# Queries, keys, values and four gate tiles of a hybrid encoder layer as seven block products

## The chip, the cores and the metric

The kernel runs on one core of a Trainium2 chip. The core has five engines with instruction streams of their own: TensorE (PE, matrix products into PSUM), VectorE (DVE), ScalarE (ACT), GpSimd (POOL) and SyncE (SP, which here only issues transfers). Work is handed from engine to engine by semaphores, and each engine runs its own instructions in order. The metric is device microseconds of one execution; 1734.17 us is the median of three runs of the kernel before (1733.97 to 1736.21).

## The reference

One layer runs over 1024 prompt tokens and 32 sample tokens, all in float32. What matters here is its first half:

```python
ada = silu(c) @ w_ada + b_ada             # six vectors of 1024; the first two make shift and gain
h = rms_norm(x, g_pre_mix) * (1 + sc1) + sh1
p = h @ w_in                              # 1024 x 4256
q_lat, c_kv, k_r, q_b, k_b, v_b, g_a, g_b = split(p)   # 384, 256, 32, 3 x 512, 2 x 1024
o_b = stick_breaking(q_b, k_b, v_b)       # 8 heads of 64, strictly causal, by a product scan
o_a = latent_attention(q_lat, c_kv, k_r)  # softmax
merged = sigmoid(g_a) * (o_a @ w_proj_a) + sigmoid(g_b) * (o_b @ w_proj_b)
```

Then follow an output projection, a residual, a convolutional feed-forward network and a second residual. The keys and values of both groups of tokens are outputs too.

## The kernel before

**Precision.** A float32 matrix is split into a high part that PE takes in one pass (`hi`, L65, an ACT copy) and the rest (`lo`, L68, a DVE subtraction). A product is then three matmuls: high by high, high by low, low by high (`mm3`, L72 to L74). "Tokens" below are the 1056 columns of the transposed activations, 1024 of the prompt and 32 of the sample.

**The opening** (`stage_h`). Eight tiles of x (128 tokens by 1024) and the 8 MB of `w_ada` for the first two vectors come in over SP's queue: the shift and gain for the first 512 features (`ada_half(0)`), then for the second 512 (`ada_half(1)`), each from eight loads of 512 KB. The pool for them has eight buffers, and the last two loads of the second half take buffers of the weight pool. ACT squares x (L105), POOL makes the reciprocal root (L97, L98), DVE scales x (L344). `norm_T` turns four tiles of x at a time by PE transposes (L281), applies gain and shift on ACT while it evacuates PSUM (L287), and makes the high and low parts on DVE (L290, L291). The result is kept whole: `hh` and `hl`, 8 blocks of 128 features by 1056 tokens.

**Projections.** `w_in_tile` loads 128 columns of `w_in` (512 KB) and splits them. `mtile` then runs 8 feature blocks by three token blocks of 352 (`BLK`) by three matmuls, 72 matmuls for one column tile.

**Stick-breaking attention** (`stage_sb`, `sb_pair`). For each of four pairs of heads there are three column tiles: queries, keys, values. The high and low parts of queries and keys go straight into the tiles the scores read; keys and values are also turned back to natural order (L400) and stored as outputs, and the values' parts are made from that. Then `sb_attend` runs the two heads by `ORDER`, a list of steps written out by hand: scores (`S`), two sigmoids on ACT (`a`, `e`), a product scan on DVE (`c`), a product on DVE (`x`), transposes (`T`), their high and low parts (`h`, `v`) and the product with the values (`V`). Between these, `f` is one step of a filler, `gates`: four gate tiles for each pair, three matmuls of 352 columns for one `f`, and now and then a step that multiplies a block of `w_ada` (`ada_step`, L203) for the four vectors wanted later. `G` copies a finished gate block out, `W` and `w` split the next gate weights, `D` is a late piece of ada.

**What sets the order.** Outside of written blocks a planner orders each engine's instructions at build time, by program order and by what it believes to be ready. Inside a written block (`manual_schedule`) PE, ACT and DVE keep the order of the text; POOL and SP are still planned, and instructions from outside the block may be put between. A pool with `bufs=n` lets n tiles of one tag live at a time; the instruction that fills the next one waits until the oldest is no longer read.

**The neighbours.** `stage_lat` projects the latent columns with `mtile`; softmax attention, merge, up projection (`stage_up`) and down projection follow. The up projection is already done by seven block products: L1687 to L1689 are its matmuls, with token blocks of 256 and 272.

## Time and profile before

| | |
|---|---|
| median of three runs | 1734.17 us |
| the profiled execution | 1733.63 us |
| its span, first to last instruction | 1731.5 us |
| TensorE busy in the span | 1691.4 us, 98%, 11518 matmuls |
| VectorE, ScalarE, GpSimd busy | 1207.4, 911.7, 283.9 us |
| bytes moved | 223.62 MB, 129 GB/s on the mean |
| first score matmul of each head pair, from the span's start | 83.1, 199.6, 321.9, 437.1 us |

The busy time of PE is the union of its matmuls, each with its latency, so a row of matmuls that follow each other without a gap is 100% busy whatever its rate. Stretches are given in microseconds from the first instruction.

### The profile page before, as it was taken

The numbers are of one execution on the slowest core, as the hardware profiler recorded it, in microseconds if no ns is written. First come the engines' busy times: TensorE is split into PE (matmuls) and PEld (weight loads), VectorE is DVE, ScalarE is ACT, GpSimd is POOL, SyncE is SP. The second block draws the span as 40 slices with busy tenths as digits, with TensorE's granted clock in tenths as the row PEclk, the third lists the DMA queues.
The fourth block names the chain that finished last, engine by engine and source line by source line (L and its number), as shares of the span: only waits on it lengthen the run. The fifth ranks groups of instructions, "written<-read, shape, count | busy, mean of one in ns | idle before, by whom it ended". The sixth has DMA issues, their size and how long they took to land. (4 is left out here: it accounts for less than half of the span.)

```text
span 1731.5 us, 29721 instructions
## 1 busy us (share of the span) xinstructions
PE 1691.4 (98%) x11518; PEld 1542.4 (89%) x11518; DVE 1207.4 (70%) x1971; ACT 911.7 (53%) x1748; POOL 283.9 (16%) x586
## 2 busy tenths in 40 slices
PE   6999999999999999999999999999999999999998
PEld 3899999999999988989889789999999999977886
DVE  4576574673663687767786679887787787778456
ACT  5454453553554666766784286444444444544442
POOL 2211110211120011101100043211111121110013
PEclk8999999999999999999999999999999999999999
DMA  8343333333342222222345531534323323697743
GB/s 322 90 132 96 108 107 97 106 113 92 112 122 68 65 65 64 75 59 68 138 143 175 184 130 37 165 104 129 129 92 128 128 92 128 212 334 248 241 147 121
DMA packets 170093, 223.62 MB, mean 129 GB/s; under 512 B 12917, under 2 KB 117056, under 8 KB 169952
## 3 DMA queue, kind: packets, MB, share of 16 engines
q1 hardware_dynamic: 154336, 177.91, 32.4%
q0 software_dynamic: 15392, 43.74, 7.1%
q8 instruction: 90, 1.47, 0.4%
q14 instruction: 51, 0.42, 0.1%
q10 hardware_dynamic: 224, 0.09, 0.0%
HBM read 169.92 MB, written 51.25 MB: 128 GB/s over the span
## 5 line engine op out<-in xcount | busy, mean ns | idle before, releaser
L65 ACT ACTIVATE wh<-wr 128x1024 fp32r<-128x1024 f32 (+6 forms) x158 | 133.8, 856 | 249.6 <-PE s L1688 78.8
L68 DVE TENSOR_TENSOR wl<-wr,wh 128x1024 fp32r<-128x1024 f32 (+5 forms) x155 | 152.7, 991 | 139.6 <-ACT wh L65 139.0
L72 PE MATMUL mm<-hh,wh 128*128 128x352 f32 x688 | 231.6, 337 | 0.0
L73 PE MATMUL mm<-hl,wh 128*128 128x352 f32 x688 | 224.2, 326 | 0.4 <-DVE hl L291 0.3
L74 PE MATMUL mm<-hh,wl 128*128 128x352 f32 x688 | 224.2, 326 | 0.0
L72 PEld LDWEIGHTS mm<-hh,wh 128*128 128x128 f32 x688 | 130.0, 189 | 9.0 <-issue 4.9
L73 PEld LDWEIGHTS mm<-hl,wh 128*128 128x128 f32 x688 | 130.0, 189 | 3.9 <-DVE hl L291 1.8
L74 PEld LDWEIGHTS mm<-hh,wl 128*128 128x128 f32 x688 | 129.7, 189 | 0.8 <-issue 0.8
L68 DVE TENSOR_TENSOR PTl<-tr,PTh 128x512 fp32r<-128x512 f32 x100 | 68.3, 687 | 50.3 <-ACT PTh L65 49.9
L1689 PE MATMUL s<-T,wl 128*128 128x256 f32 (+1 forms) x328 | 93.6, 285 | 0.0
L1687 PE MATMUL s<-T,wh 128*128 128x256 f32 (+1 forms) x328 | 93.2, 284 | 0.0
L1688 PE MATMUL s<-T,wh 128*128 128x256 f32 (+1 forms) x328 | 93.2, 284 | 0.0
L1828 DVE SCALAR_TENSOR_TENSOR u<-u,c,u 128x1058 f32<-128x1058 f32 x68 | 87.0, 1317 | 2.0 <-ACT u L1825 0.7
L65 ACT ACTIVATE PTh<-tr 128x512 fp32r<-128x512 f32 x100 | 59.4, 598 | 53.5 <-PE tr L591 50.8
L591 PE MATMUL tr<-c,A 128*128 128x128 f32 x576 | 83.6, 274 | 0.6 <-DVE A L693 0.5
L1689 PE MATMUL tr<-T,wl 128*128 128x272 f32 (+1 forms) x272 | 77.6, 285 | 0.4 <-DVE wl L68 0.4
L1687 PE MATMUL tr<-T,wh 128*128 128x272 f32 (+1 forms) x272 | 77.9, 287 | 0.0
L1688 PE MATMUL tr<-T,wh 128*128 128x272 f32 (+1 forms) x272 | 77.5, 285 | 0.0
L68 DVE TENSOR_TENSOR wl<-S,wh 128x1024 fp32r<-128x1024 f32 x40 | 48.9, 1223 | 37.4 <-ACT wh L65 36.2
L591 PEld LDWEIGHTS tr<-c,A 128*128 128x128 f32 x576 | 68.1, 140 | 5.9 <-issue 1.6
L1689 PE MATMUL mm<-T,wl 128*128 128x256 f32 (+1 forms) x256 | 73.0, 286 | 0.3 <-DVE wl L68 0.2
L1687 PE MATMUL mm<-T,wh 128*128 128x256 f32 (+1 forms) x256 | 73.1, 286 | 0.0
(694 smaller groups left out, 5391.4 us busy)
## 6 DMA issues: line engine op xcount, KB each, us to landing
wr<-in_w_ada_dram SPq DMA_DIRECT2D x48, 512.0 KB, 4.6
wr<-in_w_up_dram SPq DMA_DIRECT2D x44, 512.0 KB, 4.2
dr<-in_w_down_dram SPq DMA_DIRECT2D x43, 512.0 KB, 5.9
wr<-in_w_in_dram SPq DMA_DIRECT2D x33, 512.0 KB, 4.6
wr<-gdn SPq DMA_DIRECT2D x30, 512.0 KB, 4.2
gdn<-u POOLq DMA_DIRECT2D x23, 512.0 KB, 5.3
gd<-nat POOLq DMA_DIRECT2D x48, 176.0 KB, 2.3
t<-gd SPq DMA_DIRECT2D x16, 528.0 KB, 6.3
```

Of the source, the lines that this page charges most:

```text
L65: self.nc.scalar.activation(out, in_, AF.Identity, scale=scale)
L68: return self.nc.vector.tensor_tensor(out, full, hi.bitcast(F32), ALU.subtract)
L72: m(ps, lh, rh, start=start, stop=False)
L73: m(ps, lh, rl, start=False, stop=False)
L74: self.pe = m(ps, ll, rh, start=False, stop=stop).ins
L591: self.nc.tensor.transpose(tr[:, (2 * s + q) * P : (2 * s + q + 1) * P], at[q][:, b * P : b * P + P], self.idt)
L1687: m(ps[:, :n], w[0][:, k], x[0][:, k, c], start=first and k == 0, stop=False, skip_group_check=True)
L1688: m(ps[:, :n], w[0][:, k], x[1][:, k, c], start=False, stop=False, skip_group_check=True)
L1689: i = m(ps[:, :n], w[1][:, k], x[0][:, k, c], start=False, stop=k == 3, skip_group_check=True)
L1828: nc.vector.scalar_tensor_tensor(y, u[:, w : w + YW], self.cvT[:, w, cc : cc + 1], y, ALU.mult, ALU.add)
```

## The change

Sixteen column tiles of `w_in`, twelve for queries, keys and values and four gate tiles, are taken in eight pairs (`PAIRS`). For one pair the weights are a 2 by 2 block matrix (two column tiles by two halves of 512 features), and so are the activations (two halves of features by two halves of 528 tokens, `B11`, `B12`, `B21`, `B22`). The 2 by 2 by 2 block product takes seven products of blocks in place of eight, with sums of weight blocks (`sum_1`, `sums_w`, `sum_4`) and sums of activation blocks (`T1` to `T4`). One product has 4 feature blocks, two token blocks of 256 and 272 columns (`Z_BLK`) and three matmuls each: 24.

The first two pairs (`g0`: two gate tiles; `g1`: queries and keys of head pair 0) run in the opening, in a written order in two blocks, one in `stage_h` and one in `stage_in`. The products that need the first 512 features alone stand ahead of `ada_half(1)`. The other six pairs run in `stage_in`, outside of a written block. All four head pairs' queries, keys and values are made there, ahead of the attentions; their high and low parts go to scratch in device memory (`z_done`) and come back for each pair (`sb_load`), all on POOL's queue. `B12` is kept as plain float32 in scratch during this, and split when the last pair is done.

The attentions follow each other without projections between; the filler now has the remaining twelve gate tiles, three for each attention, with four token blocks of 264 (`HBLK`), and `ORDER` is another list. It has 104 `f` steps as before. The latents take blocks of 264 too.

Smaller edits: `ada_half` takes its weights from five buffers; the load of b_ada stands behind that of its weights; some zero fills and copies move from DVE to POOL; the rope table is loaded after the first attention; the late vectors are made in `stage_in`.

```diff
     def ada_half(self, hf, wp, tp):
...
-            last = hf == 1 and k >= KT - 2
-            w = self.tl(*((self.W, [P, 1024]) if last else (wp, [P, 2 * 512])), F32, "wr").rearrange("p (v n) -> p v n", v=2)
+            w = self.tl(wp, [P, D], F32, "wr", 5).rearrange("p (v n) -> p v n", v=2)
...
+    def norm_T(self, t0, xs, tp, hf):
...
+        if t0 < 8:
+            edge = self.tl(tp, [P, 4, 16], F32, "edge") if t0 else None
+            for k in range(4):
...
+                put(f, x, q)
+                if H:
+                    put(H[0][:, k, c], x, q)
+                    self.lo(H[1][:, k, c], f, H[0][:, k, c])
+                if t0:
+                    put(edge[:, k], tr[:, 0:16], q)
...
     def stage_h(self):
...
+            g0, g1 = self.group(0), self.group(1)
+            with tc.manual_schedule(engines={E.PE, E.Activation, E.DVE}):
+                self.ada_half(0, wp, tp)
+                self.raw_a(g0)
+                for t in range(4, 8):
+                    load(t)
+                self.raw_a(g1)
+                nc.vector.tensor_scalar(xs, xs, self.rstd_s(xs, tp), None, ALU.mult)
+                n = norm(0, 0)
+                each(n, n)
+                wa = self.unit(g0["ra"][:, :512])
+                each(n, n)
+                for t in range(4, 8):
+                    scale(t)
+                each(norm(8, 0))
+                wb = []
+
+                def later(b):
+                    if b:
+                        return
+                    n = norm(4, 0)
+                    each(n, n, n, n)
+                    for i in range(2):
+                        nc.gpsimd.dma_start(self.f12d[i], self.F[0][i])
+                        x = self.F[1][i]
+                        self.plus(x, self.F[0][i], B11, i, ALU.subtract)
+                        if i == 0:
+                            wb.append(self.unit(g1["ra"][:, :512]))
+                        self.both(T1, x, i)
+
+                g0["q1"] = self.z_q("q1", 3)
+                self.z_out(g0["q1"], self.z_prod(wa, B11, "mm mm", then=later))
+                wa, = wb
+                g1["q1"] = self.z_q("q1", 3)
+                self.z_out(g1["q1"], self.z_prod(wa, B11, "mm mm"))
+                self.ada_half(1, wp, tp)
+                self.raw_b(g0)
+                self.raw_b(g1)
+                n, m = norm(0, 1), norm(4, 1)
+                each(n, n)
+                w = [self.unit(self.sum_1(g0))]
+                each(n)
+                w.append(self.unit(self.sum_1(g1)))
+                for g, t in ((g0, "mm mm"), (g1, "s pv")):
+                    b = self.z_prod(w.pop(0), T1, t, then=lambda i: each(n if g is g0 else m))
+                    self.out_b(g, b)
+                    self.sums_w(g)
+                    w.append(self.unit(g["ra"][:, 512:]))
...
+                        self.z_half(x, B21, b, g["Y"][b], True)
...
+    def raw(self, g):
+        return self.tl(self.W, [P, 1024], F32, "wr") if g["n"] % 2 == 0 else self.tl(self.Zq, [P, 1024], F32, "S", 2)
...
+    def unit(self, x):
+        if self.n_unit % 2 == 0:
+            self.wt = [self.tl(self.W, [P, 1024], F32R, t) for t in ("wh", "wl")]
+        i = 512 * (self.n_unit % 2)
+        self.n_unit += 1
+        h, l = (t[:, i : i + 512] for t in self.wt)
+        self.hi(h, x)
+        self.lo(l, x, h)
...
+    def z_half(self, w, x, b, ps, new):
+        c0, n = self.Z_BLK[b]
+        for k in range(4):
+            for i, (p, q) in enumerate(((0, 0), (0, 1), (1, 0))):
+                self.nc.tensor.matmul(ps[:, :n], w[p][:, k], x[q][:, k, c0 : c0 + n], start=new and k + i == 0,
+                                      stop=k == 3 and i == 2, skip_group_check=True)
...
+    def step_e(self, g):
+        self.z_prod(self.unit(g["rb"][:, :512]), self.Z["T3"], None, g["X"])
+        g["ub"] = self.u_tile()
+        self.z_out(g["ub"][:, HC:], g["X"], g["q5"])
+
+    def step_f(self, g):
+        self.z_prod(self.unit(g["rb"][:, 512:]), self.Z["T4"], None, g["X"])
+        self.z_out(g["ub"][:, :HC], g["X"], g["q1"])
+        self.z_done(g["cols"][1], g["ub"])
...
+    def stage_in(self):
...
+        def t2(i):
+            self.plus(F2[i], F1[i], Z["B11"], i, ALU.add)
+            self.both(Z["T2"], F2[i], i)
...
+        with self.tc.manual_schedule(engines={E.PE, E.Activation, E.DVE}):
+            vec(F1[0], F2[0], F1[0], ALU.subtract)
+            _, p0 = seventh(g1, "tr tr")
+            t2(0)
+            vec(F1[1], F2[1], F1[1], ALU.subtract)
+            p0()
+            _, p1 = seventh(g0, "s pv")
+            t2(1)
+            p1()
+            w0 = self.unit(g0["ra"][:, :512])
+            for i in range(2):
+                self.both(Z["T3"], F1[i], i)
+            w1 = self.unit(g1["ra"][:, :512])
+            fourth(g0, w0, "tr tr")
+            for i in range(2):
+                b = [x.bitcast(F32)[:, 2 * i : 2 * i + 2] for x in Z["B21"]]
+                vec(F2[i], b[0], F2[i], ALU.subtract)
+                vec(F2[i], F2[i], b[1], ALU.add)
+                self.both(Z["T4"], F2[i], i)
+            fourth(g1, w1, "s pv")
+            self.step_e(g0)
+            self.step_f(g0)
+            self.step_e(g1)
+            self.step_f(g1)
+        for n in range(2, len(self.PAIRS)):
+            g = self.group(n)
...
+    HBLK = tuple((264 * i, 264) for i in range(4))
...
+    def sb_load(self, p):
...
+            dma(Q[r], qh[r])
+            dma(Q[o], ql[r])
+            dma(KH[lo], kh[r])
+            dma(KH[hi], kh[r])
+            dma(KL[r], kl[r])
+            ops.append((Q, KH, KL))
+        V = self.tl(self.Sp, [P, 8, 2, P], F32R, "V", 1)
+        dma(V, self.vd[p])
...
     def gates(self, ms):
...
+            for i, m in enumerate(ms):
                 wh, wl = w.pop(0)
-                yield from self.ada_step(2, self.W, self.At, ada)
-                for b, (c0, n) in enumerate(self.BLK):
+                for b, (c0, n) in enumerate(self.HBLK):
+                    if b == 2:
+                        yield from self.ada_step((3, 3, 2)[i % 3], self.W, self.At, ada)
...
     def stage_sb(self):
...
+        self.fill = self.gates(range(4, 16))
         for p in range(4):
             self.sb_pair(p)
...
     def run(self, upto=99):
         self.consts()
         self.stage_h()
+        self.stage_in()
         self.att_pools()
         self.stage_sb()
```

482 lines of the change are left out of this document (307 added, 175 removed).

## The prediction

> **What bounds the kernel now.** I read the page's head and slices first, then busy time by stage, then TensorE's timeline.
>
> ```profile
> span 1731.5 us, 29721 instructions
> PE 1691.4 (98%) x11518; PEld 1542.4 (89%) x11518; DVE 1207.4 (70%) x1971; ACT 911.7 (53%) x1748; POOL 283.9 (16%) x586
> PE   6999999999999999999999999999999999999998
> ```
>
> TensorE (PE) is full everywhere but in the first slice, so a microsecond of matmul taken away is worth a microsecond, as long as PE does not come to wait elsewhere. Columns of the next rows: stretch, then busy time (instructions) of PE, weight loads, VectorE (DVE), ScalarE (ACT), GpSimd (POOL), then granted clock, DMA share, GB/s.
>
> ```profile
> 0.00:46.50 46.50, 29.05 (x207) 16.46 (x208) 19.74 (x45) 22.39 (x36) 11.84 (x29) 0.89 0.83 304
> 15.00:20.00 5.00, 4.38 (x53) 2.09 (x45) 0.56 (x1) 0.00 (x0) 0.00 (x0) 1.00 1.06 394
> 83.10:162.40 79.30, 79.30 (x566) 74.26 (x565) 58.45 (x90) 43.04 (x94) 15.90 (x42) 1.00 0.40 120
> 162.40:199.60 37.20, 37.18 (x235) 36.60 (x233) 11.38 (x16) 12.44 (x24) 4.14 (x6) 1.00 0.27 78
> 600.00:650.00 50.00, 48.27 (x335) 43.61 (x336) 43.14 (x103) 36.82 (x89) 6.62 (x12) 1.00 0.27 76
> 1200.00:1300.00 100.00, 100.00 (x833) 99.09 (x832) 77.60 (x116) 47.48 (x77) 16.84 (x46) 1.00 0.32 104
> ```
>
> The second to last two rows are one attention with its gate fillers, the three projections after it, a softmax attention, and the up projection, which is already done by seven products. Busy time of a matmul contains its latency; its price is the distance between starts:
>
> ```profile
> 62.10 0.33 PE L73 MATMUL mm<-hl,wh 128*128 128x352 f32 x1
> 65.67 0.32 PE L74 MATMUL mm<-hh,wl 128*128 128x352 f32 x1
> 1250.10 0.28 PE L1687 MATMUL s<-T,wh 128*128 128x256 f32 x1
> 1253.03 0.28 PE L1687 MATMUL mm<-B,wh 128*128 128x256 f32 x1
> ```
>
> Between the first two lie 22 matmuls of 352 columns: 3.57/22 = 0.1623 us each. Between the last two lies one product, 12 matmuls of 256 and 12 of 272 columns: 2.93 us, 0.1221 each. By column that is 0.461 and 0.463 ns: narrow blocks cost nothing extra.
>
> **The change part by part.** *Seven products.* Two column tiles now take 2 x 72 matmuls, 23.4 us; as a group, 7 x 2.93 = 20.5. Eight groups save 8 x 2.86 = 22.9. The twelve remaining gate tiles and five latent tiles go from 72 x 0.1623 = 11.69 to 96 x 0.1221 = 11.72; 17 tiles and the rope key give back 0.6. Net -22.3.
>
> *Splits and sums.* A group needs seven half-tile splits, four half-tile weight sums and five evacuations on DVE, all of which in the middle groups lies beside 20.5 us of PE:
>
> ```profile
> L1779 DVE TENSOR_TENSOR S<-wr 128x512 f32<-128x512 f32 x1 | 0.7, 681 | 0.0
> L1764 DVE TENSOR_TENSOR u<-s,q 128x256 f32<-128x256 f32 x2 | 0.8, 418 | 0.0
> L805 POOL DMA_DIRECT2D gd<-nat x11 | 6.1, 558 | 16.1 <-ACT nat L804 16.1
> ```
>
> That is 11 x 0.68 + 5 x 0.84 = 11.7 us, 13 to 14 with the splits of queries, keys or values: 65%, less than the 77.6% under which the up projection keeps PE at 100%. Cost 0; without that cover it is what the opening pays below. The late vectors, the rope table and b_ada only move to where nothing waits for them, and the zero fills go from DVE to POOL before the first attention: 0. POOL takes eleven loads for each pair, 11 x 0.56 = 6 us beside its 15.9 of 79.3; hidden while the attention runs.
>
> *The opening* decides. Before:
>
> ```profile
> 20.04 0.64 PE L252 MATMUL s<-wr,cT 128*32 128x256 f32 x8 [0.67 <-DMA wr<-in_w_ada_dram]
> 43.08 1.50 PE L252 MATMUL s<-wr,cT 128*32 128x256 f32 x24
> 45.33 0.41 PE L72 MATMUL s<-hh,wh 128*128 128x352 f32 x1
> L73 PE MATMUL mm<-hl,wh 128*128 128x352 f32 x8 | 4.0, 498 | 0.4 <-DVE hl L291 0.3
> ```
>
> The two halves of w_ada are multiplied by 20.7 and 44.6. From 45.3 PE has no gap, and 24 projection matmuls (8 of each of three lines, to 45.3) are done: 3.9 us. PE has lost 45.3 - 3.9 = 41.4. The new opening is written out, so PE, ACT and DVE each keep its order. I add it up with these rows:
>
> ```profile
> 27.46 1.06 ACT L105 ACTIVATE jk<-x 128x1024 f32<-128x1024 f32 x1
> 28.50 1.06 ACT L105 ACTIVATE jk<-x 128x1024 f32<-128x1024 f32 x1
> 33.66 0.77 ACT L287 ACTIVATE hh<-tr,c,c 128x512 fp32r<-128x512 f32 x1
> 34.32 0.78 ACT L287 ACTIVATE hf<-tr,c,c 128x512 f32<-128x512 f32 x1
> L299 ACT ACTIVATE hf<-tr,c,c 128x32 f32<-128x32 f32 x8 | 2.4, 379 | 0.5 <-DVE hl L291 0.5
> 29.03 0.61 POOL L98 TENSOR_TENSOR rs<-rv,c 128x1 f32<-128x1 f32 x1
> 28.15 0.75 DVE L344 TENSOR_SCALAR x<-x,rs 128x1024 f32<-128x1024 f32 x1 [0.72 <-POOL rs L98]
> L65 ACT ACTIVATE wh<-wr 128x1024 fp32r<-128x1024 f32 x2 | 2.1, 1056 | 10.4 <-DMA wr<-in_w_in_dram 10.4
> L427 ACT COPY big<-s 128x352 f32<-128x352 f32 x1 | 0.5, 453 | 0.0
> L1883 DVE TENSOR_TENSOR f<-f,B 128x1024 f32<-128x1024 f32 x2 | 2.4, 1218 | 0.0
> L68 DVE TENSOR_TENSOR T<-f,T 128x1024 fp32r<-128x1024 f32 x10 | 12.0, 1221 | 0.1
> wr<-in_w_ada_dram SPq DMA_DIRECT2D x48, 512.0 KB, 4.6
> ```
>
> (a) From 20.7: 2 us to the gains, then ACT has 8 evacuations at 0.66, half a weight split 0.55, four squares at 1.04, four sample pieces at 0.3: 11.2, and some 1.9 for the last rstd on POOL and the scaling (0.61, 0.75, a second small POOL instruction and hand-overs): 35.5. Four transposed tiles with their edges, 4 x 0.93: 39.5. DVE then has four sum passes, a split and half a split, ACT the last high part: 4.9 + 1.2 + 0.7 + 1.1 = 7.9, about 1 of hand-overs: 49. Only then, in ACT's order, the first product's two banks are copied (0.8); the second product has no other bank, takes 2.93, and the second half's w_ada matmuls stand behind it on PE: 52.5, where before they had ended at 44.6.
>
> (b) These weights have five buffers now, not ten. Three of eight loads are issued as the first matmuls free buffers, about 53: 4.6 to landing, 1.33 for each further one (0.5 MB at 394 GB/s): all done at 61.
>
> (c) Gains at 62.5. ACT has 16 evacuations, 8 small ones, four half splits, four copies: 10.6 + 2.4 + 2.2 + 1.6 = 17, and waits in order for products to copy, some 6: 85. PE runs four products, 11.7 of 22.
>
> (d) From 87 DVE is the path: 16 passes for the four operand sums and their splits (19.5), five half splits (3.4), eight evacuations (3.4), four waits for ACT's high part (4.2), hand-overs: 32. The fifth product's weights come behind this in DVE's order, at 119. PE runs four products meanwhile.
>
> (e) Fifth and sixth product of both groups: each waits for the evacuation of the one before and its own weights' low part on the same DVE: 2.93 + 0.42 + 0.68 + 0.15 = 4.2, four times: 135.5.
>
> By 135.5 PE has run 14 products (41.0) and some 3 of transposes that before still came after 45.3: 91.5 lost, 50 more than before. The planner may put in later groups, but their raw weights share the buffers of these two, which come free at about 102 and 123: the third group's first three products, 9. Opening: +41. Bounds: +8, if (c) to (e) were all covered and the second half came at 50; +56, if the first half's last three loads also fall behind four of x and one of w_in on SP's queue, since they wait for buffers (5 x 1.33: 20.7 becomes 27) and nothing is put in.
>
> *Before the first attention* its operands come through scratch, into memory that the last group's fourth and fifth products free; two products (5.9) cover five issues (2.8) and a landing:
>
> ```profile
> gdn<-u POOLq DMA_DIRECT2D x23, 512.0 KB, 5.3
> ```
>
> +2; bounds 0 to 8, all eleven issued before any lands. *Attentions*: the 104 fillers stay, 96 of them with 3 x 264 columns for 3 x 352: 96 x 0.12 = 11.7 of 79.3 is the share of the saving that falls here. DVE keeps some 55 of its 58.45 (less two value splits as in the next row, their copies and one weight split) in 67.6: 82%.
>
> ```profile
> L463 DVE TENSOR_TENSOR V<-nat,V 128x512 fp32r<-128x512 f32 x2 | 1.4, 687 | 0.0
> ```
>
> The nearest row, the softmax attention's with 86% DVE, loses 3.5% of PE: 0 to 2.4 each, 0 to 9 in all; I take +2, since the order was spaced anew for shorter fillers. The value tile has one buffer: its load after the last product has 5 tail fillers, 17 more and six scores, 9 us, before it is needed. Hidden.
>
> **Sum**: -22.3 + 41 + 2 + 2 = +22.7. The profiled execution took 1733.6 (span 1731.5, 2.1 around it; 0.5 under the median): 1756.
>
> **Rivals.** *Faster.* The written order overlaps as meant: the planner fills PE's holes from later groups, and the opening costs 8: 1733.6 - 22.3 + 8 + 2 = 1721. For it: instructions from outside a written block are interleaved now, as the value transposes behind an attention's first scores:
>
> ```profile
> 83.10 0.42 PE L473 MATMUL s<-KH,Q 128*128 128x384 f32 x1
> 83.53 0.27 PE L400 MATMUL tr<-c,big 128*32 128x128 f32 x1
> ```
>
> Against: the shared raw buffers, and DVE with nothing to spare in (d). It turns faster once the opening costs under 18.
>
> *No change*: opening 15 to 22, by half of this: 1733.
>
> *Slower still, by the clock.*
>
> ```profile
> 20.00:25.00 5.00, 2.51 (x19) 1.56 (x19) 2.97 (x8) 3.23 (x4) 0.00 (x0) 0.93 1.05 404
> 30.00:35.00 5.00, 4.31 (x20) 2.31 (x21) 3.99 (x6) 2.62 (x5) 0.62 (x2) 0.61 1.05 405
> ```
>
> After PE stood half idle the granted clock fell to 0.61. At such a clock 2.93 becomes 4.8; some six products on the path (the second of (a), one of (d), four of (e)) add 11: 1767. The Trainium skill, "TensorE: Matmul & The Clock Gate", section on the HAM clock gate, has the array at half rate after one idle window of about 3.4 us until it was busy as long; by that rule only what follows holes over 3.4 us suffers, less than this rival says.
>
> *It saves nothing*: weight loads stand at 99% in the up projection, and if they bound the 168 matmuls of a group at 0.139 us, the opening alone is left: 1779. The distance of 0.122 speaks against it.
>
> **How the numbers follow.** Forecast 0.55, its own range 1740 to 1768; faster 0.25; no change 0.08; the clock 0.10; no saving 0.02. A measurement of this kernel tells about 0.2%, 3.5 us, from no change: faster 0.25, same 0.08, slower 0.67. Range 1722 to 1772: it takes in most of the faster case and half of the clock's.
>
> **What would show it.** Right: the second half's w_ada matmuls end near 60; slices 2 and 3 of PE under 9, DVE near 10 there; PE waits for `wl` and `T` from DVE at 85 to 135; afterwards PE full, attentions of some 68 to 70 us back to back, and the latents starting some 20 us later than now. Wrong: PE full from 60 on with matmuls of the third group between those of the first two (then 1721), attentions that stay at 79, or starts 0.139 apart.

## The result, and the profile after

The changed kernel takes 1818.98 us (median of 4 runs, 1814.72 to 1820.39) against 1735.19 for the kernel before on the same chip: 1.048 times as long, 95% interval 1.046 to 1.050. The forecast was 1756 with a range of 1722 to 1772: slower was right, the size was not. The page's head and slices of the changed kernel:

```profile
span 1818.6 us, 31405 instructions
PE 1707.0 (94%) x12136; PEld 1548.5 (85%) x12136; DVE 1280.2 (70%) x2103; ACT 931.2 (51%) x1816; POOL 335.6 (18%) x679
PE   5659997999999999999999999999999999999997
DVE  3466565777877458786777768977877877788556
PEclk9789899999999999999999999999999999999999
```

A slice is 45.5 us. TensorE (PE) is now short of full in the first three slices and in the seventh, and a little in the last. VectorE (DVE) stands at 4 and 6 tenths in the second and third slice, where the prediction had it near 10: it is not the engine that is full there. No engine is. Busy time by stage (stretch, then PE, weight loads, DVE, ACT, POOL, granted clock, DMA share, GB/s):

```profile
29.30:150.40 121.10, 76.90 (x487) 67.02 (x485) 66.26 (x97) 47.07 (x88) 14.08 (x19) 0.82 0.26 85
181.00:197.00 16.00, 13.01 (x59) 10.99 (x58) 3.99 (x9) 0.41 (x2) 4.97 (x9) 0.68 0.32 75
197.00:290.60 93.60, 92.85 (x757) 91.43 (x756) 59.53 (x100) 36.90 (x71) 31.99 (x50) 1.00 0.54 174
290.60:298.80 8.20, 0.56 (x6) 0.37 (x4) 2.13 (x6) 0.00 (x0) 5.50 (x14) 0.82 1.11 290
298.80:375.90 77.10, 71.84 (x555) 65.12 (x556) 54.13 (x83) 39.81 (x91) 21.00 (x52) 0.93 0.76 191
375.90:447.40 71.50, 70.29 (x573) 63.63 (x572) 54.35 (x86) 41.73 (x96) 19.05 (x48) 1.00 0.71 190
447.40:521.70 74.30, 71.37 (x581) 65.15 (x581) 57.82 (x95) 41.13 (x96) 18.03 (x47) 1.00 0.54 138
521.70:591.20 69.50, 67.95 (x561) 62.40 (x560) 53.96 (x86) 40.34 (x94) 14.53 (x39) 1.00 0.45 133
```

The rows are: the opening; a hole among the middle groups; the middle groups themselves, full; a stall before the first attention; and the four attentions, each from its first score to the next one's. From these and the trace of before the difference of the two profiled spans, 87.1 us, can be put together:

| term | predicted | measured | measured how |
|---|---|---|---|
| seven products, narrow blocks | -22.3 | -22.3 | by their unit prices, below |
| opening, first two groups | +41 | +61 | all 14 products done at 148.5 with 2 us of work of later groups; predicted 135.5 with 9 us of it |
| late vectors | 0 | +10 | last product at 290.7; at 280.9 with them moved away |
| before the first attention | +2 | +8 | 290.6 to 298.8 |
| four attentions | +2 | +18 | 292.4; before 432.8 (83.1 to the rope key at 515.9), less three stretches of projections at 37.2 and four gate tiles at 11.7: 274.4 |
| latents | within +0.6 | +3 | rope key to first softmax score, 103.6 against 100.8 |
| softmax stage | 0 | +3 | granted clock near 0.5 for some 7 us at one place |
| end of the kernel | 0 | +6 | last VectorE instruction to the end, 9.1 against 3.5 |

These add up to 87. The first line's unit prices: the last product of a steady group begins at 287.65 and the filler behind it at 290.59, 2.94 us for 24 matmuls (2.93 before); the filler's matmuls of 264 columns start 0.12 apart.

```profile
287.65 0.41 PE L514 MATMUL s<-H,wh 128*128 128x256 f32 x2
290.59 0.29 PE L81 MATMUL mm<-H,wh 128*128 128x264 f32 x1
290.71 0.29 PE L82 MATMUL mm<-H,wh 128*128 128x264 f32 x1
```

So the saving is there, and five times as much is lost elsewhere. The opening, as the waits of PE between 29.3 and 150.4 (what it waited for: total, times, longest) and as some of its instructions:

```profile
PE tr L514 <- ACT wh L74: 15.1, 3, 12.8
PE mm L514 <- ACT q L522: 7.5, 1, 7.5
PE s L259 <- DMA wr<-in_w_ada_dram: 4.0, 3, 2.4
```

```profile
51.31 0.58 PE L514 MATMUL mm<-H,wh 128*128 128x256 f32 x1 [7.53 <-ACT q L522]
57.59 1.39 SPq L256 DMA_DIRECT2D wr<-in_w_ada_dram  x3
64.58 0.66 PE L259 MATMUL s<-wr,cT 128*32 128x256 f32 x4 [0.93 <-DMA wr<-in_w_ada_dram]
93.75 1.25 DVE L611 TENSOR_TENSOR u<-u,u 128x1056 f32<-128x1056 f32 x1
118.89 1.08 ACT L74 ACTIVATE b12h<-u 128x1056 fp32r<-128x1056 f32 x1 [6.20 <-DVE u L627]
130.03 0.80 PE L514 MATMUL tr<-H,wh 128*128 128x256 f32 x2 [12.77 <-ACT wh L74]
148.42 0.29 PE L514 MATMUL pv<-b12h,wl 128*128 128x272 f32 x1
```

At 51.31 the second first product starts, having waited 7.5 us for ScalarE's copies; at 57.59 the last three loads of w_ada are issued; from 93.75 VectorE makes T2 to T4; at 130.03 PE starts the fifth product after 12.8 us without a matmul; at 148.42 the last matmul of the fourteenth product starts.

In the hole at 181 to 197 the late vectors are loaded one small transfer after another. PE waits 3.0 us for them in all, and VectorE's copy of their transposes stands in its queue ahead of the next weight splits. PE's matmuls then run at half clock from 186.6 to 196.8, after a stretch in which PE was busy 1.32 of 3.4 us; that is worth some 5 of the 10 us (an estimate: half of 9.9 us busy).

```profile
181.59 1.56 POOL L157 DMA_DIRECT2D hs<-in_conv_w_dram  x3
192.34 0.33 PE L159 MATMUL tr<-c,hs 44*128 44x44 f32 x1
192.71 0.17 DVE L172 COPY c<-tr 128x13 f32<-128x13 f32 x1 [5.92 <-PE tr L159]
```
```profile
183.20:186.60 3.40, 1.32 (x8) 0.83 (x7) 0.58 (x2) 0.00 (x0) 2.77 (x4) 1.00 1.14 305
186.60:196.80 10.20, 9.90 (x39) 8.58 (x40) 2.42 (x6) 0.02 (x1) 0.00 (x0) 0.50 0.05 12
```

The waits of PE from 286 to 376, before and in the first attention, are for transfers but for 0.2 us; the longest:

```profile
PE s L760 <- DMA KH<-khd: 7.6, 1, 7.6
PE mm L212 <- DMA wr<-in_w_ada_dram: 3.1, 1, 3.1
PE pv L883 <- DMA V<-vd: 1.5, 1, 1.5
```

### The profile page after: what moved, and what is told of

It reads as the page before. It is cut to its first block, busy times and chain, and to the rows that moved or that the text cites. A ratio compares the mean times of both kernels' runs of the same rounds, so it can differ in the third digit from the quotient of the medians.

```text
span 1818.6 us, 31405 instructions
## 1 busy us (share of the span) xinstructions
PE 1707.0 (94%) x12136; PEld 1548.5 (85%) x12136; DVE 1280.2 (70%) x2103; ACT 931.2 (51%) x1816; POOL 335.6 (18%) x679
## 3 DMA queue, kind: packets, MB, share of 16 engines
q0 software_dynamic: 22720, 72.09, 12.4%
## 5 line engine op out<-in xcount | busy, mean ns | idle before, releaser
L74 ACT ACTIVATE wh<-wr 128x1024 fp32r<-128x1024 f32 (+5 forms) x166 | 131.6, 804 | 247.6 <-PE s L1971 72.5
L81 PE MATMUL mm<-H,wh 128*128 128x264 f32 x348 | 102.5, 294 | 0.0
L83 PE MATMUL mm<-H,wl 128*128 128x264 f32 x348 | 99.7, 286 | 0.0
L82 PE MATMUL mm<-H,wh 128*128 128x264 f32 x348 | 99.3, 285 | 0.0
L1972 PE MATMUL s<-T,wl 128*128 128x256 f32 (+1 forms) x328 | 93.7, 286 | 0.0
L77 DVE TENSOR_TENSOR wl<-S,wh 128x1024 fp32r<-128x1024 f32 (+1 forms) x64 | 65.1, 1021 | 36.1 <-ACT wh L74 34.6
L77 DVE TENSOR_TENSOR PTl<-tr,PTh 128x512 fp32r<-128x512 f32 x100 | 68.2, 686 | 29.9 <-ACT PTh L74 29.3
L74 ACT ACTIVATE wh<-S 128x1024 fp32r<-128x1024 f32 (+1 forms) x64 | 57.0, 897 | 50.5 <-PE s L1971 12.7
L830 DVE TENSOR_TENSOR_SCAN M<-M,tab 128x512 f32<-128x512 f32 (+4 forms) x64 | 58.6, 916 | 27.2 <-ACT M L815 27.0
L2101 POOL COPY c<-u 128x2 f32<-128x2 f32 x44 | 25.5, 579 | 265.0 <-DVE u L2047 230.2
L869 PEld LDWEIGHTS tr<-c,A 128*128 128x128 f32 x576 | 65.7, 141 | 9.2 <-DVE PTl L77 1.9
```

Source lines behind the costliest of these rows:

```text
L74: self.nc.scalar.activation(out, in_, AF.Identity, scale=scale)
L77: return self.nc.vector.tensor_tensor(out, full, hi.bitcast(F32), ALU.subtract)
L81: m(ps, lh, rh, start=start, stop=False)
L82: m(ps, lh, rl, start=False, stop=False)
L83: self.pe = m(ps, ll, rh, start=False, stop=stop).ins
L830: self.nc.vector.tensor_tensor_scan(r, r, tab[:, ::-1], 0.0, ALU.mult, ALU.max)
```

## The experiments

All ratios are to the kernel before, with their 95% interval; "products end" is when the last block product of the eight groups ends, 290.7 in the changed kernel. The ratios of e1, e3, e4, e5, e15 and e17 overlap with the changed kernel's (1.046 to 1.050), so these runs are read by the stretches of their traces, one trace each. In three traces with the same opening (the changed kernel, e2, e15) the products end within 0.6 us of each other.

**e3, T4's sums later in the written order.**

```diff
             fourth(g0, w0, "tr tr")
-            for i in range(2):
...
-                self.both(Z["T4"], F2[i], i)
             fourth(g1, w1, "s pv")
             self.step_e(g0)
-            self.step_f(g0)
             self.step_e(g1)
+            for i in range(2):
...
+                self.both(Z["T4"], F2[i], i)
+            self.step_f(g0)
             self.step_f(g1)
```

> In the written order the sums of the sixth product's operand (T4: four passes and two splits on VectorE) come after the fourth products of both groups and after both fifth products, instead of ahead of the second group's fourth. Theory A: TensorE has the two fifth products (5.9 us) and their waits inside the hole of 117 to 130, and the first raw loads of later groups come earlier: time falls by 5 to 8, to about 1812. Rival B (VectorE is the path through the whole stretch, the same passes in another order end at the same time): within 3 us of 1819.

1824.25 us (1.0515, 1.0494 to 1.0537); products end at 292.1. The fifth products do come earlier (120.4, not 130.0), and the sixth later (140.2, not 135.9): nothing is won by this. Rival B for the products; the time is 5 us longer than in the changed kernel, 2 more than Rival B allows.

**e4, memory for all eight loads of w_ada's second half** (that of B22). **e5, the second half early in the order as well**: the second of the two edits; the call stood behind both first products.

```diff
-            w = self.tl(wp, [P, D], F32, "wr", 5)
+            w = self.yb.pop() if hf == 1 and k >= KT - 3 else self.tl(wp, [P, D], F32, "wr", 5)
```
```diff
                     n = norm(4, 0)
                     each(n, n, n, n)
+                    self.ada_half(1, wp, tp)
```

> The last three loads of w_ada's second half get memory of their own (that of the block B22, which is written later), so that all eight are issued without waiting for matmuls. Theory A: the second half's matmuls follow directly on the second first product, end at about 60 instead of 65.7 us, and everything behind moves up by 5 to 6: 1813. Rival B (what follows is bound by VectorE and by waits for later things): less than 2 us.

> As the run with all eight loads of w_ada's second half issued at once, and in addition the second half's matmuls, its transposes and its vectors stand in the written order ahead of the second first product, right after the transposes of the second four tiles of x. Theory A (in the first 70 us TensorE and ScalarE wait for the second half of w_ada): its matmuls end at about 47 instead of 60.5, the first product with the sums (T1) starts some 8 to 10 earlier than the 74 of that run, the last block product ends near 278, and the time is near 1805. Rival B (VectorE's chain of sum passes sets the end of the opening): the last block product ends within 2 us of 287, the time stays near 1813.

e4: 1813.16 us (1.0471, 1.0449 to 1.0493), w_ada's second half done at 60.5, products end at 287.0. e5: 1813.66 (1.0457, 1.0439 to 1.0476), done at 45.7, products end at 284.4. Of 20 us by which the weights came earlier, 6 reached the end: in e4 3.7 of 5.2, in time what Theory A had; in e5 only 2.6 more, Rival B. The trace of e5 shows what else stood there:

```profile
54.56 1.08 ACT L74 ACTIVATE H<-u 128x1056 fp32r<-128x1056 f32 x1 [3.79 <-DVE u L463]
55.96 0.80 PE L520 MATMUL mm<-H,wh 128*128 128x256 f32 x2 [7.73 <-ACT q L528]
60.96 0.38 PE L288 MATMUL tr<-c,b12l 128*128 128x128 f32 x2
```

PE waits for the copy of the first product's banks, the copy stands on ScalarE behind T1's second high part, that waits for VectorE's pass; and the transposes for the second half, whose vectors were ready at 47, stand behind that product on PE.

**e17, T1's sums behind both first products (with e5).**

```diff
                 def later(b):
...
-                    for i in range(2):
...
-                        self.both(T1, x, i)
...
                 self.z_out(g1["q1"], self.z_prod(wa, B11, "mm mm"))
...
                 n, m = norm(0, 1), norm(4, 1)
                 each(n, n)
+                sums_1()
```

> As the run with the second half of w_ada early in the written order, and one move more: the four sum passes and splits of T1 stand behind both first products and behind the second half's first two normalised tiles, no longer between the first product and the copy of its result. There TensorE waited 7.7 us for ScalarE's copy, ScalarE for VectorE's passes, and 64 transposes stood behind. Theory A (this order in ScalarE's and TensorE's queues, not the weights of w_ada, made the first stretch cost 27 us): the wait goes, the second first product runs near 48 instead of 56, the first product with T1 starts near 60 instead of 66, the last block product ends some 6 to 10 earlier than 284.4: time 1804 to 1808. Rival B (the passes are only needed later and the chain on VectorE keeps its length): the last block product ends within 2 of 284.4, time 1812 or more.

1811.78 us (1.0430, 1.0404 to 1.0457), products end at 284.6. The wait of 7.7 is gone, and the first product with T1 waits 12.4 for its weights' high part instead and starts at 65.9, as in e5 (66.4). Rival B again: in e3, e5 and e17 a wait was moved, and each time another took its place.

**e8, three products more in the hole, nobody reads them.**

```diff
             fourth(g1, w1, "s pv")
+            for _ in range(3):
+                self.z_prod(w1, Z["T2"], "mm mm")
             self.step_e(g0)
```

> Three products more, whose result nobody reads, stand on TensorE in the hole of 117 to 130 us (8.8 us of matmuls with operands that are there). Theory A (after the hole TensorE starts at a granted clock of 0.6, and that costs time): the fifth product behind it runs at 0.122 instead of some 0.21 per matmul, TensorE's work ends 1.5 to 2 earlier there. Rival B (the products behind the hole wait for VectorE anyway): the last block product ends within 0.5 us of 290.7.

One run, 1821.37 us; products end at 291.0. The three products end at 126, the fifth starts at 130 as before, and the clock has fallen all the same:

```profile
120.00:126.00 6.00, 6.00 (x50) 5.85 (x48) 4.77 (x4) 1.09 (x2) 0.00 (x0) 1.00 0.01 3
125.30:128.70 3.40, 0.77 (x7) 0.55 (x5) 2.23 (x5) 0.37 (x1) 1.29 (x1) 1.00 0.00 0
128.70:130.00 1.30, 0.00 (x0) 0.00 (x0) 0.59 (x1) 1.30 (x4) 0.32 (x1) 0.50 0.00 0
130.00:136.00 6.00, 5.50 (x25) 5.21 (x26) 1.67 (x3) 1.58 (x4) 0.77 (x2) 0.54 0.43 175
```

The end is within the 0.5 us of Rival B, but Theory A's condition, a full clock at the fifth product, never came about. So what the clock costs in total isn't told by this run; that it falls within 4 us without a matmul, after 8.8 us of full work, is. The Trainium skill, "TensorE: Matmul & The Clock Gate", section "What's actually happening", says half rate after one idle window of about 3.4 us; here it fell 2.6 us after the last matmul ended (126.07), so a shorter gap was enough.

**e6, e13, e14: the written order taken away**, for both stretches (e6), for the first alone (e13: norms, first products, T1, third products; the first hunk), for the second alone (e14: T2 to T4 and the rest; the second hunk).

```diff
-            with tc.manual_schedule(engines={E.PE, E.Activation, E.DVE}):
+            if True:
                 self.ada_half(0, wp, tp)
...
-        with self.tc.manual_schedule(engines={E.PE, E.Activation, E.DVE}):
+        if True:
             vec(F1[0], F2[0], F1[0], ALU.subtract)
```

> The two stretches with a written order (first and second groups) are left to the planner, the instructions are the same. Theory A (the written order sets the waits of the opening): the planner fills the hole at 117 to 130 from later groups, the last block product ends 10 or more earlier than 290.7, time 1808 or less. Rival B (the data of the opening, weights of w_ada first and then VectorE's sums, set its length under any order): the last block product ends between 285 and 297 and the time stays within 6 of 1819.

> Only the first written stretch (norms, first products, T1, weight sums, third products, up to 100 us) is left to the planner; the second (seventh and fourth products, T2 to T4, fifth and sixth products) keeps its order. Both together had saved 37 us. Theory A (the second half of the opening, where the products stand behind VectorE's sums, holds most of it): 1819 falls by 10 to 15. Rival B (the first stretch holds most, since the second only follows VectorE): by 25 or more.

> Only the second written stretch is left to the planner. Theory A: the hole at 117 to 130 is filled with products of later groups or with fifth and sixth products, 1819 falls by 20 to 25. Rival B: by 10 or less.

| | us | ratio | products end |
|---|---|---|---|
| both (e6) | 1781.81 | 1.0282 (1.0251 to 1.0312) | 253.9 |
| first stretch (e13) | 1791.75 | 1.0354 (1.0314 to 1.0393) | 265.6 |
| second stretch (e14) | 1802.76 | 1.0405 (1.0373 to 1.0438) | 275.5 |

The same instructions in the planner's order end 37 us earlier, Theory A of e6. The first stretch alone gives 25 of them (27 us of time, Rival B of e13), the second 15 (16 us of time, between the two theories of e14). Busy time in e6 and in the changed kernel, 60 to 80 and 80 to 100 us:

```profile
60.00:80.00 20.00, 17.26 (x136) 16.43 (x135) 17.80 (x28) 17.31 (x35) 3.28 (x2) 1.00 0.00 1
80.00:100.00 20.00, 12.44 (x68) 11.50 (x67) 18.97 (x24) 5.71 (x9) 4.31 (x5) 0.70 0.32 87
```
```profile
60.00:80.00 20.00, 13.26 (x80) 10.39 (x81) 7.19 (x14) 8.00 (x13) 0.94 (x1) 0.66 0.17 65
80.00:100.00 20.00, 13.91 (x95) 12.80 (x94) 13.53 (x23) 9.37 (x20) 2.05 (x2) 0.91 0.00 1
```

VectorE is busy 36.8 of 40 us in the planner's order, 20.7 in the written one. The two kernels do not do the same work in these stretches, but in e6 VectorE is nearly full (and PE falls to 12.4 of 20), while in the written order all three engines wait for each other in turn.

**e1, the late vectors back in the first attention. e11, their loads early and their transposes late** (on e10 below).

```diff
-            if n == 2:
-                self.late_vectors()
...
     def sb_pair(self, p):
...
+        if p == 0:
+            self.late_vectors()
```

> The vectors that are needed late (nine small loads on GpSimd's queue, seven transposes on TensorE, two copies on VectorE) move from behind the third group to the first attention, where they stood before the change. Theory A (the time is lost at separate places, each a wait in an in-order queue): the hole of TensorE at 181 to 197 us goes, about 11 us of the 13.98 us that the middle groups lose, and the time falls from 1819 to about 1808. Rival B (VectorE or the raw weights bound the groups there, and the transposes only show where PE happened to wait): another wait takes its place and the time stays within 3 us of 1819.

> As the plain opening, but the nine loads of the late vectors are issued right behind w_ada's second half, and their transposes stand behind the second plain tile, so that neither the products nor the first attention meet a load that is on its way. Theory A (the transposes cost 2 us of TensorE, and the rest of what they cost anywhere is waiting for their own small loads): the first attention is 4 to 5 shorter, the products no longer than 2 more: 2 to 3 less than the plain opening. Rival B: same time within 1.5.

e1: 1812.97 us (1.0463, 1.0443 to 1.0482). The products end at 280.9, 9.8 earlier; but the four attentions take 297.6 instead of 292.4, since PE now waits 4.3 us for one of the small loads there. Half the gain is given back, and the time lies between the two theories. e11: 1761.45 against 1763.51 of e10 in the same comparison; the first attention is 2.6 shorter, the products end 2.0 later. In e10 PE waits 10.0 us for a small load in the first attention, in e11 10.8 us for VectorE: another wait takes its place there. The time falls by the 2 us of Theory A, but the first attention gains only 2.6 of the 4 to 5 that it had.

**e2, the attentions' operands through SyncE's queue.**

```diff
-        dma = self.nc.gpsimd.dma_start
+        dma = lambda x, y: self.nc.sync.dma_start(x.bitcast(F32), y)
```

> The eleven loads of each attention's operands go through SyncE's queue instead of GpSimd's. Theory A: before the first attention they no longer stand behind the stores of the last group on GpSimd (two waits of about 2.1 us) nor take 0.55 us each there; the stall of 8 us falls to about 4, and the long drain of GpSimd at the end, 10.4 us against 4.8 before the change, becomes shorter, because 44 fewer transfers were issued there: together 1819 to about 1810. Rival B (the transfers' bytes bound the stall: 3.5 MB at some 300 GB/s are 11 us): the stall stays at 7 to 8, and if the drain has nothing to do with the number of transfers the time stays at 1819.

1807.33 us (1.0429, 1.0413 to 1.0446). From the last product to the first score 0.2 us instead of 8.1; the first attention waits 4.6 for w_ada in its place, so that last product to second attention shrinks from 85.2 to 74.0. So the first score did not wait for the bytes, as Rival B had it, but for the queue: Theory A. Part of the gain went to w_ada's transfers; 3.5 us of the time came from GpSimd's drain at the end, 6.9 instead of 10.4.

**e9: e1, e2 and e6 together. e10: with a plain opening.** In e10 the first four gate tiles go through eight products, and T1 to T4 are formed beside them, with their order left to the planner.

```diff
+            for c0 in self.PAIRS[0] + self.PAIRS[1]:
+                w = self.w_in_tile(c0)
+                for h, X in enumerate(((B11, B21), (B12, B22))):
+                    q = self.z_q("q1", 3)
+                    for b, t in enumerate(("mm", "s")):
...
```

> Three edits together: the opening's order left to the planner, the operands' loads on SyncE's queue, the late vectors in the first attention. Theory A (the waits are separate, their prices add): 1782 - 12 - 6 = 1764. Rival B (what one edit saves is the same wait that another saves): 1772 or more.

> As the three edits together, and the first two groups are plain: the four first gate tiles go through eight block products (16 half products of 24 matmuls for each pair, 23.4 us in place of 20.5), which need no sums, and the sums T1 to T4 for the six later groups are formed beside them; the memory of B22 takes three loads of w_ada. TensorE has 5.9 us more to do. Theory A (the opening lost its time because its products wait for the chain of sum passes on VectorE, some 27 us with their splits): TensorE's products end near 235 (ideal work 182 us, with before's 41.4 and some 10 lost), and the time is 1740 to 1750. Rival B (the opening is bound by the weights of w_ada and by VectorE whatever it multiplies): the products end near 250, 1760 or more.

e9: 1769.49 us (1.0188, 1.0163 to 1.0213), products end at 247.1; the prices add to within 6, between the two theories. e10: 1763.51 (1.0154, 1.0131 to 1.0176), products end at 243.6 although PE has 5.9 us more to do. From 80 to 120 us PE is at 20.00 of 20, so the sums no longer stop it; but the end is 8 later than Theory A had it, and the time is Rival B's: either part of the opening's loss isn't the sums, or the 10 us that Theory A allowed for other losses were too few. No run tells which.

**e12, e15: one more buffer for w_ada in the attentions** (on e11, and alone). **e16: e12 with one plain pair instead of two**, the other gates as the last group.

```diff
-            w = self.tl(pool, [P, D], F32, "wr")
+            w = self.tl(self.Sp, [P, D], F32, "wa", 1) if i == 1 else self.tl(pool, [P, D], F32, "wr")
```

> As the run before it, and of the two or three tiles of w_ada that follow each other in an attention the second has a buffer of its own, so three in place of two are on their way. The attentions of the changed kernel wait 9.6 us in all before w_ada's matmuls beyond those of before. Theory A (two buffers for three loads in a row cause it): 4 to 7 less than the run before it. Rival B (bandwidth while the operands of the next attention load): within 1.5 of it.

> The changed kernel, where in each attention the second of the two or three tiles of w_ada in a row has a buffer of its own. Theory A (the attentions wait for w_ada because of two buffers): the four attentions, 292.4 from first score to rope key, become 286 to 288, the time 1813 to 1815. Rival B: 1819, attentions 291 or more.

> As the plain opening with the buffer for w_ada, but only the first pair of gate tiles is plain, the other gates are the last group again, by seven products. TensorE has 2.95 us less to do; and the last group stores two gate tiles (1.1 MB) instead of query and key (2 MB and two stores of low parts) just before the first attention, whose memory waits for those stores (an 11 us stall). Theory A: the stall falls to 4 or less, the opening loses up to 5 more because T1 to T4 have 23 us of cover instead of 47: 1745 to 1752. Rival B (T1 to T4 need the cover of two pairs): 1757 or more.

e15: 1810.39 us (1.0450, 1.0422 to 1.0478); the attentions take 287.7 instead of 292.4. e12: 1756.95 (1.0116, 1.0094 to 1.0138), 4.5 less than e11. Both fit the buffers, Theory A: PE's waits before w_ada's matmuls fall from 6.8 us in the changed kernel's attentions to 2.6 in e15. In e12 PE waits once, early in the first attention:

```profile
PE tr L834 <- DVE A L787: 11.0, 1, 11.0
```

VectorE stood still for 8.9 us there, while the last group's four stores of query and key were under way, 10.5 to 11.9 us from issue to landing. In e16, whose last group stores gates, that stall is gone (first attention 74.0 instead of 80.9) and the opening is longer (products end at 251.4 instead of 243.8): 1755.86 (1.0127, 1.0110 to 1.0144), the same time, between its two theories. Why VectorE stood still in e12 is not shown beyond this. None of these versions beats the kernel before.

**e7, the kernel before with four blocks of 264 in latents and rope key.**

```diff
-                for c0, n_, ps in self.mtile(wh, wl, self.Hh, self.Hl, self.BLK, KT, "mm s s"):
+                for c0, n_, ps in self.mtile(wh, wl, self.Hh, self.Hl, self.HBLK, KT, "mm s s"):
```

> The kernel before the change, with four blocks of 264 columns in place of three of 352 in the five latent tiles and the rope key alone. The kernel after the change takes 2.8 us more from the rope key to the first softmax score, and 3 us more in one place of the softmax stage, where the granted clock falls to 0.5 for some 10 us. Theory A (the fourth block brings one more chain for the root of the mean squares, with 14 in place of 12 matmuls that sum): 1734 becomes 1737, and the stretch grows from 100.8 to about 103.6; if the clock falls at the same place in the softmax stage too, the blocks are its cause and the time is 1740. Rival B (narrow blocks cost only their matmuls, 0.2 us, and the 2.8 come from memory that moved): 1734.

1734.90 us (1.0008, 0.9993 to 1.0023): the 2.7 us of the trace lie inside that interval. Rope key to first softmax score 103.5 instead of 100.8: as in the changed kernel, so the blocks are the cause, Theory A. The query latents' norm sums eight times instead of six, and PE waits 1.9 us for VectorE there, which is most of it (of before, of the changed kernel; e7 has the same 1.9):

```profile
L865 PE MATMUL mm<-big,c 128*128 128x352 f32 x6 | 2.5, 493 | 0.0
```
```profile
L1148 PE MATMUL mm<-big,c 128*128 128x264 f32 x8 | 2.7, 421 | 1.9 <-DVE big L1285 1.8
```

The granted clock falls in the softmax stage too, at the same place, in the profile of this run and not in that of before (e7, then before):

```profile
766.00:773.00 7.00, 7.00 (x39) 6.72 (x39) 0.69 (x1) 2.79 (x7) 0.00 (x0) 0.63 0.24 65
```
```profile
763.70:770.70 7.00, 7.00 (x56) 6.50 (x55) 1.77 (x6) 3.77 (x11) 0.54 (x1) 1.00 0.29 83
```

But it stays at 1.00 there in the profiles of e5, e10 to e14 and e16, which have the narrow blocks too. So the blocks alone don't bring that loss. Whether they make it likelier stays open: it is in 11 of the 18 profiles with narrow blocks and in neither of the two with wide ones (before, e18).

**e18, the kernel before with 74 small stores more on GpSimd's queue.**

```diff
+        z = self.dr.tile([19, 16, P], F32, name=f"z{p}")
+        for i in range(19 if p < 2 else 18):
+            nc.gpsimd.dma_start(z[i], self.sel[0:16])
```

> The kernel before the change with 74 small stores more on GpSimd's queue (8 KB each, 18 or 19 ahead of each attention), as many as the change adds. At the end of every kernel GpSimd stands in a drain until nothing is left: 4.7 us with 251 transfers issued there, 6.9 with 281, 7.5 with 285, 10.4 with 325. Theory A (its length goes by the number of transfers issued on GpSimd, 0.077 us each): the drain becomes 10.4 and the time grows by 5 to 6. Rival B (it goes by bytes or packets, 43.7 MB before and 72.1 after, or by something else in the changed kernels): the drain stays under 5.5 and the time at 1733 to 1735.

1749.45 us (1.0083, 1.0068 to 1.0098). GpSimd's drain at the end becomes 10.0 us instead of 4.8, with 0.6 MB more moved on its queue: Theory A. The time grew by more, because the planner put many of the stores into the opening, where the norms wait for GpSimd (first score at 93.1 instead of 83.1).

## Why the prediction was right and wrong

*Seven products and blocks*: right, to 0.01 us a product. *Splits hidden in the middle groups*: right; VectorE stands at 59.5 of 93.6 there, 64% (65% predicted), and PE is full.

*The opening* was the right place, and its mechanisms (a) and (b) are in the trace as named: PE waits for ScalarE's copies behind T1's high parts, and three loads of w_ada are issued late (57.6, predicted 53; done at 65.7, predicted 61). The term was mis-sized all the same: +61 for +41, and outside its own bounds of +8 to +56. Of the 20, 13 are slip along the chain and 7 work of later groups that didn't come.
- The slip grows at nearly every step: the last w_ada matmuls 4.7 late (65.7 for 61), VectorE's stretch (d) begins 6.7 late (93.7 for 87), the fifth products' weights come 12 late (131 for 119), the products end 13 late (148.5 for 135.5). Step (d), "From 87 DVE is the path", had VectorE's work about right, 28.0 us for 26.3, and its waits too small; before it, VectorE is busy only 15.2 of 31.2:

```profile
93.70:130.00 36.30, 17.46 (x114) 15.73 (x114) 28.01 (x36) 11.72 (x20) 3.55 (x4) 0.84 0.15 44
62.50:93.70 31.20, 21.76 (x131) 18.71 (x131) 15.24 (x27) 16.42 (x32) 2.99 (x2) 0.73 0.03 10
```

 In the written order PE, ScalarE and VectorE wait for each other in turn, which the sum had only as 4.2 us of waits for high parts and some hand-overs. So VectorE was not the path, as e6 and e14 show: the same instructions in another order end earlier, with VectorE 92% busy (e6, 60 to 100) or full (e14, 100 to 120), and 37 and 15 us are gone. Which single pair of instructions holds it can't be said: e3, e4, e5 and e17 each took one wait away, and the products ended between 1.4 later and 3.7 earlier.
- Work of later groups in PE's holes, 9 us: 2 (17 matmuls of the third group, from 143 on). The shared raw buffers came free at 111 and 114, not 102, when the written order still had PE.
- The clock, priced as a rival at 11 us: it did fall (0.82 on the mean), and lies inside the +61; e8 couldn't separate it. On the path it shows plainly at the second product, which took 5.6 us (51.3 to 56.9) instead of 2.93. In all, PE is busy 26 us at half clock between 29 and 150, so at full clock it could have been at most 13 less (an estimate).
- Some of (a)'s subtotals don't add up (its terms give 35.8 and 48.4 where it has 35.5 and 49), by less than 1 us each.

*"The late vectors ... only move to where nothing waits for them"*: wrong by 10. The step looked for who reads the vectors, and not at whose queue the loads, transposes and copies stand in; nor did it price the half clock behind the short waits, some 5 of the 10.

*Before the first attention*: the value taken, 2, was wrong, and the upper bound, 8, is what came; the loads stood behind two stores of the last group on GpSimd's queue, and on another queue the wait before the first score went (e2).

*Attentions*: outside the bounds. The price was read off VectorE's load (82%), from the softmax attention's row. Of the 18, PE's idle time in the four rows makes 11, and the granted clock of 0.93 in the first some 5 (an estimate: 0.07 of 77.1). The longest waits are for transfers: of w_ada, 6.8 in all, which now follow in threes on two buffers (e15 gave back 4.7 with one buffer more), and of the value tile, put at hidden, 1.5. The rest is spread over many small gaps and stays open, as does what the planner would make of the attentions' own written order.

*Latents, 0.6*: mis-sized; only the matmuls were counted, not the norm's chain per block. *End of the kernel*: there was no step for it; the +6 is GpSimd's drain (e18).

*Rivals.* "Faster" and "no change" fell: the planner filled in 2 us, and the opening cost 61. "Saves nothing" fell: 0.12 apart. "Slower still, by the clock" got the side right and was too small as well. No rival had several terms go wrong at once: opening, late vectors, transition, attentions and end all erred to the same side, and a range to 1772 left no room for that.

## What to carry to other kernels

A written order costs what its longest chain through *all* engines takes, not the work of the fullest engine: where three engines hand over in turn, look for the busy share of each, and compare with the planner's order before trusting the hand-made one. A step that is moved is costed by the queues it is put into, its small loads, transposes and copies included, and not by who reads its result. A faster stage needs its transfers faster too: three loads in a row on two buffers cost 4.7 us here.

## What the runs showed of the hardware that was not expected

- GpSimd's last instruction, a drain, lasts longer the more transfers GpSimd has issued in the whole program: 4.8 us with 251, 6.9 with 281, 7.5 with 285, 10.4 with 325, and 10.0 with 325 where 74 of them were stores of 8 KB (e18). That is some 0.075 us a transfer; in e18 the number grew to that of the changed kernel and the bytes stayed (44.4 MB, with 43.7 before and 72.1 after). The third of the three numbers is the longest drain, in ns (changed kernel, before, e18):

```profile
L2514 POOLq DRAIN  x3: 46/98/10397, 1807.4 to 1818.3; - x3
```
```profile
L2230 POOLq DRAIN  x3: 46/93/4762, 1726.0 to 1731.3; - x3
```
```profile
L2233 POOLq DRAIN  x3: 46/159/9987, 1736.6 to 1747.5; - x3
```

 The last VectorE instruction of the changed kernel, and of before, in the timeline (the spans end at 1818.6 and 1731.5):

```profile
1808.05 1.41 DVE L2409 SCALAR_TENSOR_TENSOR u<-u,rs,d 128x512 f32<-128x512 f32 x2 [0.31 <-POOL rs L2407]
```
```profile
1726.60 1.41 DVE L2126 SCALAR_TENSOR_TENSOR u<-u,rs,d 128x512 f32<-128x512 f32 x2 [0.31 <-POOL rs L2124]
```

- A VectorE pass with two inputs took 1.80 us instead of 0.68 where GpSimd's addition of two tiles had started 0.06 us before it:

```profile
78.88 0.68 DVE L553 TENSOR_TENSOR wr<-wr,wr 128x512 f32<-128x512 f32 x1
```
```profile
84.72 1.32 POOL L539 TENSOR_TENSOR q<-q,q 128x528 f32<-128x528 f32 x1 [3.99 <-ACT q L522]
84.78 1.80 DVE L553 TENSOR_TENSOR S<-S,S 128x512 f32<-128x512 f32 x1
```

 The Trainium skill, "GPSIMD Engine Reference", section "Specifications", says that the two share their SBUF interfaces, with contention where a VectorE instruction has two inputs there; the rows agree and give it a size, 1.1 us. In the first row VectorE was the first, by 0.18 us: it was not slowed, and GpSimd's addition at 79.06 took 1.67 us instead of 1.32. These are two single cases.
- The granted clock can halve where PE was never idle for 3.4 us. In the softmax stage it did so for 7 to 10 us in 11 of 20 profiles, always at the same place: in eight of them PE had no gap over 0.6 us in the 20 us before, in e3, e4 and e6 one of 1.3 to 1.6, and e18 with such a gap of 1.5 kept 1.00. In the changed kernel's hole it fell at 186.6 after gaps of 1.8 us and less. The cause in the softmax stage stays open.
